# A float32 decoder trunk on one core: the down projection accumulates onto the residual held in PSUM, and one more of its weight pairs is multiplied in seven block products

## Chip, cores and metric

The kernel runs on one core of one Trainium2 chip. The metric is the device time of one execution in microseconds (us); three runs of the kernel before gave 2077.24 to 2078.20, with a median of 2077.91 us.

## What is computed

Two pre-norm residual layers over a stream `h` of 256 positions by 2048 features, all in float32. Each layer adds a mixer (sliding-window attention beside an mLSTM in the first layer, forgetting attention in the second) and then a SwiGLU feed-forward block (FFN); a last RMSNorm ends it. The change lies in the FFN:

```
def swiglu(xn, w_gate, w_up, w_down):
    return (jax.nn.silu(xn @ w_gate) * (xn @ w_up)) @ w_down
...
        h = h + swiglu(rms_norm(h, norm_ffn[layer]), w_gate[layer], w_up[layer], w_down[layer])
```

`w_gate` and `w_up` are 2048 x 5632, `w_down` is 5632 x 2048.

## The kernel before

**Numbers in two parts.** Every float32 operand is split into a part `hi`, rounded to the matrix engine's type fp32r, and the rest `lo`. A product is three matmuls into one PSUM bank, hi by hi, hi by lo and lo by hi (`three`, L508 to L511). The activations are split once and stay resident (`xh`, `xl` for the FFN's input; `mh`, `ml` for its hidden values); the weights are split as they arrive: ScalarE casts `hi` (L177, L339), VectorE subtracts `lo` (L178, L340).

**Tiles.** Weights are loaded in chunks of 256 rows by 512 columns (512 KB, `load_raw`, on SyncE's queue). The 256 positions are two halves t of 128. `pair_group` (L516) computes two column blocks of 512 at once, m = 0 and 1, for both t: four accumulators `plain[m][t]`, one PSUM bank each. It walks over pairs of k (256 rows), in an order given by a table of (kind, pair).

- A **plain pair** (kind 0) splits two chunks of 128 x 1024 and multiplies eight blocks: 24 matmuls.
- A **mixed pair** (kind 1) regards the 2 x 2 blocks of positions and the 2 x 2 blocks of weights as a block product and forms it with seven products: 21 matmuls. It needs sums of weight blocks `ta`, `tb`, `tc`, `td` (four subtractions on VectorE, L568 to L571), their split into `ht` and `lt` (two tiles each, L339 and L340), and sums of activation blocks, made once per pair and part (`sums_of`, into `sx` for the FFN's input and `sd` for its hidden values). Four of its products go into four further banks, `prods`, which all mixed pairs of a group share.

After its last mixed pair a group joins the four `prods` into the tile `c` (`combine`: one ScalarE copy L525, four VectorE additions L526 to L529).

PSUM has two pools of four banks, `pm` and `pa`. A group takes its `plain` banks from one and its `prods` from the other; the next group takes them the other way round. So a group's `plain` banks are those that the group before had as `prods`, and come free through `combine`.

**The FFN** (`ffn`, L598) runs in three parts of the hidden dimension, of 3, 4 and 4 column blocks (`PARTS`). In each part, a gate and up group per column block (eight k pairs, `ORDER`, three of them mixed) makes 512 hidden columns, which are turned, split into `mh`, `ml`, and summed for the mixed pairs of down. Then two down groups (n0 = 0 and 2) multiply the part's hidden values by `w_down`, in 6 pairs for the part of 3 blocks and 8 for the others (`DOWN`), and add into `h`. In the very last part the second down group is replaced by two plain `gemm` calls. That makes 22 gate and up groups and 11 down groups, of which 4 have six pairs and 7 have eight.

Before, a down group adds to `h` in two steps: `c` as soon as `combine` has made it (L708), then each `plain` bank when its last matmul is done (`add_out`, L353).

**Buffers.** `hi` and `lo` of whole chunks: six each (`wp`). `ht` and `lt`: two each, which is one mixed pair. Raw weights: four for plain chunks, four more for the chunks of mixed pairs. `t4`: one, for `ta` and `tb`, in the groups that pass no `halves` (the FFN's). `c`: one.

**Order.** When the kernel is built, a scheduler lays out the instructions of each engine in one sequence, and tiles carry the semaphores between the sequences. So a change in one place can move instructions in others.

Of the kernel before, what the change touches and what calls it, by code (L numbers as in the profile page):

```python
# [37 lines left out]
    6: ((0, 0), (1, 1), (0, 2), (1, 3), (0, 4), (0, 5)),  # L38
    8: ((0, 0), (1, 1), (0, 2), (1, 3), (0, 4), (1, 5), (0, 6), (0, 7)),
# [33 lines left out]
def trunk(  # L73
# [253 lines left out]
    def scrap(fp, n):  # L327
        if n % 2 == 0:
            box = fp.tile([P, 4, NB], F32, tag="c", name="box", bufs=1)
            halves = box[:, 0:2, :], box[:, 2:4, :]  # L330
        elif n == 3:
            halves = [fp.tile([P, 3, NB], F32, tag=f"sd{i}", name="box", bufs=1)[:, 0:CK, :] for i in range(2)]
# [175 lines left out]
    def three(o, ah, al, hi, lo, start, stop):  # L508
        nc.tensor.matmul(o, ah, hi, start=start, stop=False)  # L509
        nc.tensor.matmul(o, ah, lo, start=False, stop=False)  # L510
        nc.tensor.matmul(o, al, hi, start=False, stop=stop)  # L511
# [4 lines left out]
    def pair_group(fp, par, lhs, sums, mats, order, todo=(), halves=None, inner=None, raws=None):  # L516
        plain = [[bank(par, "acc") for _ in range(NT)] for _ in range(2)]
        todo = list(todo)
# [13 lines left out]
        for pos, (kind, pair) in enumerate(order):  # L532
# [4 lines left out]
            if not kind:  # L537
# [4 lines left out]
                for m, (w, c0) in enumerate(mats):  # L542
                    hi, lo = load_chunk(w, k0, c0, NB)
                    run_due(todo, pos)
                    for i, t in walk:
# [4 lines left out]
                            pos == 0 and i == 0, last and i == CK - 1,  # L550
# [3 lines left out]
            if first:  # L554
# [18 lines left out]
            for src in (ra, rb) if halves else (t4, ra):  # L573
# [8 lines left out]
            where = ((0, 0), (1, 0), (1, 1), (0, 1)) if halves else ((0, 0), (0, 1), (1, 0), (1, 1))  # L582
# [6 lines left out]
            three(plain[0][0], xb[:, t0], lb[:, t0], hg[:, 1, :], lg[:, 1, :], False, False)  # L589
            three(plain[1][0], sh[:, 3, :], sl[:, 3, :], hu[:, 1, :], lu[:, 1, :], False, False)  # L590
# [3 lines left out]
            three(plain[0][1], xb[:, t1], lb[:, t1], ht[3], lt[3], False, False)  # L594
# [4 lines left out]
    def ffn(layer, fp, sx, sd, key, todo, idx_next=None, key_next=None, finish=None):  # L599
# [6 lines left out]
        for g0, g1 in zip(PARTS, PARTS[1:]):  # L606
# [69 lines left out]
            def close(acc, n):  # L676
                if not end:
                    add_out(acc, n)
                elif idx_next is None:
                    finish(acc, n, gf)  # L680
                else:
                    add_out(acc, n)
# [8 lines left out]
            for n0 in (0, 2):  # L691
                if end and idx_next is None and n0 == 2:
                    for n in (2, 3):
                        acc = new_acc()
                        gemm(acc, m_of, wd, n * NB, NB, 0, nk, nk, skew=3 if n == 3 else 1, halved=n == 3)
                        close(acc, n)
                    continue
                plain, c = pair_group(
                    fp, 1 - n0 // 2, m_of, sums_d, [(wd, n0 * NB), (wd, (n0 + 1) * NB)], order, todo
# [5 lines left out]
                for m in range(2):  # L705
                    for t in range(NT):
                        o = h[:, t, (n0 + m) * NB : (n0 + m + 1) * NB]
                        nc.vector.tensor_tensor(out=o, in0=c[:, 2 * m + t, :], in1=o, op=ALU.add)  # L708
                for m in range(2):
                    close(plain[m], n0 + m)  # L710
# [526 lines left out]
    def finish(acc, n, gf):  # L1237
        for t in range(NT):
            half = n == 3 and t == NT - 1
            part, mean, rs = (ft[:, a, t : t + 1] for a in range(3))  # L1240
            for i in range(2 if half else 1):
                cs = slice(i * S, (i + 1) * S) if half else slice(0, NB)
                o = h[:, t, n * NB + cs.start : n * NB + cs.stop]
                nc.vector.tensor_tensor(out=o, in0=acc[t][:, cs], in1=o, op=ALU.add)
# [77 lines left out]
```

## Time and profile before

| what | value |
|---|---|
| median of 3 runs | 2077.91 us |
| span of the profiled execution | 2076.6 us |
| matrix engine (PE) busy | 2066.4 us |
| vector engine (DVE) busy | 1824.5 us |
| scalar engine (ACT) busy | 1374.7 us |
| HBM read | 408.68 MB, 198 GB/s over the span |

The span runs from the first to the last instruction of one profiled execution; the median of the runs lies 1.3 us above it. A row of the grouped view gives line, engine, operation, tile written from tiles read, shape, count, then the busy time of the group and the mean duration of one instruction. A row of the timeline gives start, duration, engine, line and operation. Two instructions that follow each other on an engine overlap at their edges, so the distance of two starts is less than the duration.

### The profile page before, as it was taken

How to read it: one execution, taken by the hardware profiler on the slowest of the kernel's cores; microseconds unless marked ns; L12 is line 12 of the kernel's file. 1: busy time of each engine (PE TensorE's matmuls, PEld its weight loads, DVE VectorE, ACT ScalarE, POOL GpSimd, SP SyncE). 2: the span in 40 equal slices, each digit the busy share in tenths (PEclk: the TensorE clock that was granted, in tenths of full speed). 3: DMA queues.
4: the chain of work that ended last, by engine and by line, in shares of the span. 5: the costliest groups of instructions: out<-in, count | busy, mean ns of one | idle time of the engine just before them, and what ended most of it. 6: DMA issues, size and time to landing. Idle time of an engine off the chain costs nothing.

```text
span 2076.6 us, 26994 instructions
## 1 busy us (share of the span) xinstructions
PE 2066.4 (100%) x9473; PEld 1715.0 (83%) x9473; DVE 1824.5 (88%) x2410; ACT 1374.7 (66%) x1736; POOL 41.7 (2%) x66
## 2 busy tenths in 40 slices
PE   9999999999999999999999999999999999999998
PEld 7878888888888888888888888888888888888887
DVE  6788769999999999999899778689999999999994
ACT  6777678765676656667676776687655667456763
POOL 1010000000000000000000001000000000000000
PEclk9999999999999999999999999999999999999999
DMA  8566577666566666666576866586665667666764
GB/s 292 172 213 188 190 247 236 203 217 206 189 230 223 205 210 205 220 212 204 185 215 204 235 193 184 156 283 220 206 205 200 213 206 234 203 202 213 220 197 138
DMA packets 309575, 434.87 MB, mean 209 GB/s; under 512 B 106412, under 2 KB 114624, under 8 KB 309312
## 3 DMA queue, kind: packets, MB, share of 16 engines
q1 hardware_dynamic: 307088, 426.27, 65.1%
q0 software_dynamic: 1632, 5.80, 0.8%
q8 instruction: 74, 1.21, 0.2%
q10 hardware_dynamic: 720, 1.09, 0.2%
q14 instruction: 61, 0.50, 0.1%
HBM read 408.68 MB, written 2.12 MB: 198 GB/s over the span
## 4 chain that ended last, share of the span: by engine, by line
PE 97%; DVE 1%; ACT 1%; DMA 1%; issue 1%; SPq 0%; POOLq 0%; POOL 0%; ACTq 0%; DVEq 0%
PE acc L510 21%; PE acc L509 21%; PE acc L511 21%; PE acc L213 5%; PE acc L212 5%; PE acc L214 5%; PE prod L509 5%; PE prod L510 5%; PE prod L511 5%; PE p L369 1%; PE po L470 1%; DMA raw<-in_w_in_odd_dram 0%; ACT s L403 0%; PE po L471 0%; DVE lo L178 0%
## 5 line engine op out<-in xcount | busy, mean ns | idle before, releaser
L177 ACT CAST hi<-raw 128x1024 fp32r<-128x1024 f32 (+3 forms) x656 | 664.8, 1028 | 440.2 <-PE acc L511 269.1
L178 DVE TENSOR_TENSOR lo<-raw,hi 128x1024 fp32r<-128x1024 f32 (+3 forms) x656 | 772.8, 1192 | 146.3 <-ACT hi L177 143.5
L510 PE MATMUL acc<-lo,xh 128*128 128x512 f32 x1254 | 488.6, 390 | 0.0
L509 PE MATMUL acc<-hi,xh 128*128 128x512 f32 x1254 | 485.9, 390 | 0.5 <-ACT hi L177 0.5
L511 PE MATMUL acc<-hi,xl 128*128 128x512 f32 x1254 | 484.8, 389 | 0.0
L510 PEld LDWEIGHTS acc<-lo,xh 128*128 128x128 f32 x1254 | 235.4, 188 | 49.4 <-DVE lo L178 0.6
L509 PEld LDWEIGHTS acc<-hi,xh 128*128 128x128 f32 x1254 | 235.2, 188 | 49.5 <-ACT hi L177 0.7
L511 PEld LDWEIGHTS acc<-hi,xl 128*128 128x128 f32 x1254 | 235.4, 188 | 48.8
L510 PE MATMUL acc<-lo,mh 128*128 128x512 f32 x437 | 169.7, 389 | 0.0
L511 PE MATMUL acc<-hi,ml 128*128 128x512 f32 x437 | 168.4, 389 | 0.0
L509 PE MATMUL acc<-hi,mh 128*128 128x512 f32 x437 | 167.9, 389 | 0.0
L339 ACT CAST hi<-raw 128x512 fp32r<-128x512 f32 x109 | 67.6, 620 | 89.4 <-PE acc L511 80.5
L213 PE MATMUL acc<-lo,mh 128*128 128x512 f32 (+1 forms) x322 | 126.3, 392 | 0.0
L212 PE MATMUL acc<-hi,mh 128*128 128x512 f32 (+1 forms) x322 | 125.8, 391 | 0.0
L214 PE MATMUL acc<-hi,ml 128*128 128x512 f32 (+1 forms) x322 | 123.7, 391 | 0.0
L340 DVE TENSOR_TENSOR lt<-t,ht 128x1024 fp32r<-128x1024 f32 x95 | 115.8, 1219 | 5.2 <-ACT ht L339 5.1
L339 ACT CAST ht<-t 128x1024 fp32r<-128x1024 f32 x95 | 99.9, 1051 | 30.7 <-PE prod L511 28.8
L339 ACT CAST ht<-raw 128x1024 fp32r<-128x1024 f32 x95 | 99.7, 1050 | 29.7 <-PE acc L511 15.0
L340 DVE TENSOR_TENSOR lt<-raw,ht 128x1024 fp32r<-128x1024 f32 x95 | 115.7, 1218 | 1.8 <-ACT ht L339 1.8
L213 PE MATMUL acc<-lo,xh 128*128 128x512 f32 (+3 forms) x288 | 99.8, 348 | 0.2 <-DVE lo L178 0.2
L214 PE MATMUL acc<-hi,xl 128*128 128x512 f32 (+3 forms) x288 | 98.1, 344 | 0.0
L212 PE MATMUL acc<-hi,xh 128*128 128x512 f32 (+3 forms) x288 | 95.9, 347 | 0.3
(363 smaller groups left out, 3448.0 us busy)
## 6 DMA issues: line engine op xcount, KB each, us to landing
raw<-in_w_gate_dram SPq DMA_DIRECT2D x176, 512.0 KB, 4.5
raw<-in_w_up_dram SPq DMA_DIRECT2D x176, 512.0 KB, 4.6
raw<-in_w_down_dram SPq DMA_DIRECT2D x176, 512.0 KB, 5.1
raw<-in_w_in_odd_dram SPq DMA_DIRECT2D x88, 512.0 KB, 4.9
raw<-in_w_in_even_dram SPq DMA_DIRECT2D x51, 512.0 KB, 5.0
raw<-in_w_out_even_dram SPq DMA_DIRECT2D x32, 512.0 KB, 5.1
raw<-in_w_out_odd_dram SPq DMA_DIRECT2D x32, 512.0 KB, 4.8
hr<-in_w_in_even_dram SPq DMA_DIRECT2D x12, 512.0 KB, 4.6
```

The lines of the kernel that those rows point to most:

```text
L177: latest[0] = nc.scalar.copy(hi[:, k, 0:n], raw[:, k, 0:n])
L178: nc.vector.tensor_tensor(out=lo[:, k, 0:n], in0=raw[:, k, 0:n], in1=hi[:, k, 0:n].bitcast(F32), op=ALU.subtract)
L212: nc.tensor.matmul(o, ah[:, ts], hi, start=(k == 0), stop=False)
L213: nc.tensor.matmul(o, ah[:, ts], lo, start=False, stop=False)
L214: nc.tensor.matmul(o, al[:, ts], hi, start=False, stop=(k == k_all - 1 and cs.stop == n))
L339: nc.scalar.copy(dst_h, src)
L340: nc.vector.tensor_tensor(out=dst_l, in0=src, in1=dst_h.bitcast(F32), op=ALU.subtract)
L369: nc.tensor.matmul(pq[j % 2][:, j // 2, :], q_of(j, b), k_of(j)[:, 0:cols], start=True, stop=True)
L470: nc.tensor.matmul(po, v_of(j, 0), tt[:, j, 0:2, :].rearrange("p c q -> p (c q)"), start=True, stop=False)
L509: nc.tensor.matmul(o, ah, hi, start=start, stop=False)
L510: nc.tensor.matmul(o, ah, lo, start=False, stop=False)
L511: nc.tensor.matmul(o, al, hi, start=False, stop=stop)
```

## The change

Six edits:

1. A down group copies its four blocks of `h` into its four `plain` banks before the first matmul (ScalarE, new L518 to L521), and the matmuls accumulate onto them; none of them starts a new sum. At the end one addition per block, `plain` + `c`, writes `h`. The addition of `c` to `h` (L708 before) and `add_out` in the down groups (L353 before) fall away.
2. In `DOWN`, a third pair of six and a fourth of eight becomes mixed, and in the group of eight the plain pair 4 moves ahead of the mixed pair 3.
3. `t4` goes. All groups now write the sums of weights in the raw tiles: `ra` holds `ta` and `td`, `rb` holds `tb` and `tc`.
4. So the split tiles hold other blocks. Before, in the FFN, the first `ht` held `ta`, `tb` and the second `tc`, `td`; now the first holds `ta`, `td` and the second `tb`, `tc`. The first is thereby used by the second and by the last of the products that take sums of weights.
5. The scrap tiles with the tags of `sd` grow to four blocks, and `sd` itself takes four pairs in place of three.
6. `finish` and `close` skip the addition where nothing is left to add.

```
 DOWN = {
-    6: ((0, 0), (1, 1), (0, 2), (1, 3), (0, 4), (0, 5)),
-    8: ((0, 0), (1, 1), (0, 2), (1, 3), (0, 4), (1, 5), (0, 6), (0, 7)),
+    6: ((0, 0), (1, 1), (1, 2), (1, 3), (0, 4), (0, 5)),
+    8: ((0, 0), (1, 1), (1, 2), (0, 4), (1, 3), (1, 5), (0, 6), (0, 7)),
 }
...
+        if base is not None:
+            for m in range(2):
+                for t in range(NT):
+                    nc.scalar.copy(plain[m][t], base(m, t))
...
-                            pos == 0 and i == 0, last and i == CK - 1,
+                            base is None and pos == 0 and i == 0, last and i == CK - 1, base is not None,
...
-            t4 = ra if halves else fp.tile([P, 2, NB], F32, tag="t4", name="t4", bufs=1)
-            ta, tb, tc_, td = (
-                (ra[:, 0, :], rb[:, 0, :], rb[:, 1, :], ra[:, 1, :])
-                if halves
-                else (t4[:, 0, :], t4[:, 1, :], ra[:, 0, :], ra[:, 1, :])
-            )
+            ta, tb, tc_, td = ra[:, 0, :], rb[:, 0, :], rb[:, 1, :], ra[:, 1, :]
...
-            for src in (ra, rb) if halves else (t4, ra):
+            for src in (ra, rb):
...
-            where = ((0, 0), (1, 0), (1, 1), (0, 1)) if halves else ((0, 0), (0, 1), (1, 0), (1, 1))
+            where = ((0, 0), (1, 0), (1, 1), (0, 1))
...
                 if not end:
-                    add_out(acc, n)
+                    return
...
-                        o = h[:, t, (n0 + m) * NB : (n0 + m + 1) * NB]
-                        nc.vector.tensor_tensor(out=o, in0=c[:, 2 * m + t, :], in1=o, op=ALU.add)
-                for m in range(2):
-                    close(plain[m], n0 + m)
+                        nc.vector.tensor_tensor(out=place(m, t), in0=plain[m][t], in1=c[:, 2 * m + t, :], op=ALU.add)
+                    close(None, n0 + m)
```

More of the change, by code (lines that the diff above doesn't have):

```diff
@@ L331, in scrap @@
         elif n == 3:
-            halves = [fp.tile([P, 3, NB], F32, tag=f"sd{i}", name="box", bufs=1)[:, 0:CK, :] for i in range(2)]
+            halves = [fp.tile([P, 4, NB], F32, tag=f"sd{i}", name="box", bufs=1)[:, 0:CK, :] for i in range(2)]
         else:
@@ L593, in pair_group @@
             three(prods[3], sh[:, 1, :], sl[:, 1, :], ht[2], lt[2], first, last)
-            three(plain[0][1], xb[:, t1], lb[:, t1], ht[3], lt[3], False, False)
+            three(plain[0][1], xb[:, t1], lb[:, t1], ht[3], lt[3], False, False, base is not None)
         if inner is None:
```

22 lines of the change are left out of this document (12 added, 10 removed).

## The prediction, made before the changed kernel ran

> **What bounds the kernel now.** I read the page first: busy time, then the chain that ended last.
>
> ```profile
> span 2076.6 us, 26994 instructions
> PE 2066.4 (100%) x9473; PEld 1715.0 (83%) x9473; DVE 1824.5 (88%) x2410; ACT 1374.7 (66%) x1736; POOL 41.7 (2%) x66
> ...
> PE 97%; DVE 1%; ACT 1%; DMA 1%; issue 1%; SPq 0%; POOLq 0%; POOL 0%; ACTq 0%; DVEq 0%
> ```
>
> The matrix engine is never idle for long: 10.2 us of the span. Matmuls overlap, so busy time hides their pace; that I take from starts in the timeline, on PE and then on VectorE, at the end of a down group:
>
> ```profile
> 1004.57 0.39 PE L511 MATMUL prod<-ht,sd 128*128 128x512 f32 x1
> ...
> 1005.03 0.39 PE L511 MATMUL acc<-ht,ml 128*128 128x512 f32 x1
> ...
> 1007.52 0.39 PE L510 MATMUL acc<-lo,mh 128*128 128x512 f32 x1
> ```
> ```profile
> 1005.00 0.69 DVE L526 TENSOR_TENSOR c<-prod,c 128x512 f32<-128x512 f32 x1 [2.26 <-PE prod L511]
> 1005.73 0.69 DVE L527 TENSOR_TENSOR c<-prod,c 128x512 f32<-128x512 f32 x1
> 1006.45 0.69 DVE L528 TENSOR_TENSOR c<-prod,c 128x512 f32<-128x512 f32 x1
> 1007.06 0.68 DVE L529 TENSOR_TENSOR c<-prod,c 128x512 f32<-128x512 f32 x1
> 1007.66 1.28 DVE L708 TENSOR_TENSOR h<-c,h 128x512 f32<-128x512 f32 x2
> ```
>
> From the start at 1004.57 to that at 1007.52 there are 13 steps in 2.95 us: one matmul is worth 0.227 us. And a reader of a bank starts 0.04 us after the last matmul's end (1004.57 + 0.39 to 1005.00). Next, the windows over the two FFN stretches (columns: PE, PE load, DVE, ACT, POOL busy, clock, DMA share, GB/s):
>
> ```profile
> 293.00:1009.00 716.00, 716.00 (x3168) 592.92 (x3167) 670.14 (x839) 469.79 (x534) 0.69 (x1) 1.00 0.66 212
> 1385.00:2025.00 640.00, 640.00 (x2829) 529.91 (x2828) 605.70 (x752) 414.41 (x457) 1.28 (x2) 1.00 0.66 211
> ```
>
> VectorE is busy for 1275.8 of 1356 us, 94.1%: the second limit is close. The waits say why it is not nearer:
>
> ```profile
> ACT hi L177 <- PE acc L511: 269.3, 187, 5.0
> ...
> DVE lo L178 <- ACT hi L177: 143.5, 166, 5.5
> ```
>
> ScalarE waits for matmuls to free `hi` tiles, and VectorE for ScalarE: both run ahead of PE until the tiles are full. PE has a lead over nothing; they have one over it.
>
> **Part 1, matmuls saved.** 29 mixed pairs of down show as 87 rows of three products each; the new tables have 4 x 3 + 7 x 4 = 40. Each of the 11 more saves three matmuls, 33 in all, and the built programs differ by just that (9301 and 9268). Gain 33 x 0.227 = **7.5 us**, on PE, which sets the end.
>
> ```profile
> L510 PE MATMUL prod<-lt,sd 128*128 128x512 f32 x87 | 33.9, 389 | 0.0
> ...
> L353 DVE TENSOR_TENSOR h<-acc,h 128x512 f32<-128x512 f32 x56 | 37.2, 683 | 4.8 <-PE acc L214 4.4 <-PE acc L511 0.4
> L708 DVE TENSOR_TENSOR h<-c,h 128x512 f32<-128x512 f32 x44 | 29.5, 684 | 0.0
> ```
>
> **Part 2, VectorE's account.** Its pace, again by starts:
>
> ```profile
> 660.83 0.68 DVE L568 TENSOR_TENSOR t<-raw 128x512 f32<-128x512 f32 x1
> 661.44 0.68 DVE L569 TENSOR_TENSOR t<-raw 128x512 f32<-128x512 f32 x1
> 662.04 1.22 DVE L340 TENSOR_TENSOR lt<-raw,ht 128x1024 fp32r<-128x1024 f32 x1
> 663.17 0.68 DVE L340 TENSOR_TENSOR sd<-s,sd 128x512 fp32r<-128x512 f32 x1
> 663.78 4.62 DVE L178 TENSOR_TENSOR lo<-raw,hi 128x1024 fp32r<-128x1024 f32 x4
> 668.32 1.22 DVE L340 TENSOR_TENSOR lt<-t,ht 128x1024 fp32r<-128x1024 f32 x1
> ```
>
> A half tile (512) takes 0.605, a whole one 1.135 us. A plain pair costs two wholes, 2.27; a mixed pair three wholes and five halves, 6.43, so one more costs 4.16, and 11 cost 45.8. The sums of activations for six more pairs (one per part) take four small additions and the `lo` of a half tile each; the small ones follow at 0.21:
>
> ```profile
> 656.11 0.29 DVE L262 TENSOR_TENSOR s<-c 128x128 f32<-128x128 f32 x1
> 656.32 0.28 DVE L264 TENSOR_TENSOR s<-c 128x128 f32<-128x128 f32 x1
> ```
>
> That is 4 x 0.2 + 0.605 = 1.4 per pair, 8.4 for six. The one addition per block in place of two saves 44 x 0.605 = 26.6. Net **+27.6 us**: the FFN then needs 1303.4 of 1348.5 us, 96.7%, if PE keeps its pace. In a six-pair down group the account is 30.95 us of VectorE (9 wholes, 15 halves in the three mixed pairs with 6 wholes more, 8 halves) against 135 x 0.227 = 30.6 of PE: there it lives on its lead.
>
> **Part 3, ScalarE.** 44 copies of `h`, and 1.6 us of casts per extra mixed pair, some 50 us in all on an engine that is two thirds busy: nothing in bulk. The write into PSUM has no row; the nearest are the copy out of it and the cast in SBUF.
>
> ```profile
> L525 ACT COPY c<-prod 128x512 f32<-128x512 f32 x40 | 23.1, 577 | 0.0
> ...
> L339 ACT CAST hi<-raw 128x512 fp32r<-128x512 f32 x109 | 67.6, 620 | 89.4 <-PE acc L511 80.5 <-ACT ht L339 4.3 <-issue 2.9
> ```
>
> I take 0.62 and keep 0.58 to 0.70 as bounds; over the five places below where it counts, that is 0.2 us down and 0.4 up. The Trainium skill ("ScalarE: Activation LUTs", section "Step-by-step: what each stage is for") holds that ScalarE reaches PSUM faster than SBUF, without a figure for this form; by it the low end would stand, 0.2 us off the sum.
>
> **Part 4, where PE will wait.** The order of the changed program differs in all FFN groups, not in down alone. Before, the last `prods` matmul of a group stands some 25 to 55 places ahead of the first `plain` matmul of the next; at the first eight-pair down group 40, or 9.07 us:
>
> ```profile
> 667.72 0.39 PE L511 MATMUL prod<-ht,sx 128*128 128x512 f32 x1
> ...
> 676.79 0.39 PE L509 MATMUL acc<-hi,mh 128*128 128x512 f32 x1
> ```
>
> After the change it is the tail of the group:
>
> ```
> 3009 L511 Matmult prod_5835<-ht_6018,sx1_2411 128x512
> 3010 L509 Matmult acc_6148<-hi_6245,mh_60 128x512
> 3011 L510 Matmult acc_6148<-lo_6246,mh_60 128x512
> 3012 L511 Matmult acc_6148<-hi_6245,ml_61 128x512
> 3013 L509 Matmult acc_6149<-hi_6158,mh_60 128x512
> ```
>
> `acc_6149` takes the bank of `prod_5835`. It needs that product's end, the first addition of `combine`, and now a copy of `h`. On ScalarE the copy stands behind the cast of an `ht` tile that the same row 3009 frees. Casts follow at 0.94:
>
> ```profile
> 656.89 1.04 ACT L339 CAST ht<-t 128x1024 fp32r<-128x1024 f32 x1
> 657.83 1.05 ACT L339 CAST mh<-c 128x1024 fp32r<-128x1024 f32 x1
> ```
>
> So: matmul 0.39, 0.04, cast 0.94, copy 0.62, 0.05, together 2.04 us; four places give 4 x 0.227 = 0.91. PE waits 1.13. Queued behind the copy is the cast of the next `hi`, and behind PE's wait everything. There are four such boundaries (the gate to down step of all eight-pair parts), 4.5 us, and one with seven places, 0.45. The rest by the same way of counting:
>
> - Turn to layer 1: the transposes of `h` that need a block with `c` stand six places (1.36 us) behind the last `prods` matmul; in between lie its end 0.43, four `combine` additions (1005.00 to 1007.66, 2.66 us) and the block's addition 0.69, 3.8 us. Wait **2.5**. Before, 48 places lay between.
> - One reuse of an `ht` tile after 3 places (0.68) where end, cast and hand-over take 1.53: 0.85. Two of an `lt` tile after 10 places (2.27) with a subtraction more (2.79): 1.0. One `hi` after 4: 0.6.
>
> These chains begin and end on PE, so no lead elsewhere shortens them: **9.9 us**. Beyond them some 40 reuses (first banks of gate groups with 7 to 9 places, `lo` and `lt` with 15 to 17, `ht` and `hi` with 9 to 11) have less than 1 us over their chain. If a quarter of them finds ScalarE or VectorE half way through an instruction of 1.05 to 1.22, that is 10 x 0.55 = **5.5 us**, an estimate from those rows.
>
> Of the rest: the raw tiles that now hold the sums are freed with the last `lt`, as `ra` was before, and SyncE loads `ra` ahead of `rb`, so the weight stream doesn't start later; no DMA is added. Without `t4` a first `ht` waits for four subtractions in place of two, 1.2 us, hidden by the lead of `lt`:
>
> ```profile
> 658.36 1.22 DVE L340 TENSOR_TENSOR lt<-t,ht 128x1024 fp32r<-128x1024 f32 x1
> ```
> ```profile
> 663.64 0.39 PE L510 MATMUL prod<-lt,sx 128*128 128x512 f32 x1
> ```
>
> Made at 659.58, read at 663.64: 4 us early. If that cover goes, 11 pairs of down lose up to 1.2 us each, 13 us; that belongs to the second rival.
>
> **Sum.** 2076.6 - 7.5 + 9.9 + 5.5 = 2084.5 us for the profiled execution's span; the median of the runs shown is 1.3 higher, and I set the forecast between, **2085**.
>
> **Rivals.**
>
> 1. *PE stays the limit (the other side).* The order is pessimistic: also in the old order matmuls with `lt` are split off and put late, and the trace shows those tiles 4 us early. If PE then arrives late at the tight places because it is itself the slow one, or the chains overlap with waits that I count twice, the 33 matmuls come out whole: 2077.9 - 7.5 = 2070.4. It decides as long as all waits stay under 7.5 us. Against it: the chains start at PE's own row.
> 2. *VectorE becomes the limit.* If it can't be pushed over today's 94.1%, the FFN takes 1303.4 / 0.941 = 1385 us in place of 1356: 2077.9 + 29 = 2107. It decides once the lead of about 4 us is used up in the down groups. For it: the six-pair groups' account; against it: the 9.9 us of waits on PE give VectorE time back.
> 3. *Gain and chains cancel*, without the queueing: 2077.9 - 7.5 + 9.9 = 2080.3, to 2077 if ScalarE's copies are early.
> 4. *The clock falls* where PE pauses. If it halved for the first pair (24 matmuls) of each down group: 11 x 24 x 0.227 = 60, 2138. The rows show a clock of 1.00 in both stretches. The Trainium skill ("TensorE: Matmul & The Clock Gate", section "HAM oscillation — how this bites in real kernels") puts the pause that does it at over some 3.4 us; the waits counted here are shorter.
>
> **Chances.** Forecast (2080.5 to 2095) 0.55; rival 1 (2070 to 2076) 0.19; rival 2 (2095 to 2110) 0.13; rival 3 (2076 to 2080.5) 0.12; rival 4 0.01. A difference of 0.2%, 4.2 us, is about what this kernel's measurement can tell: faster means under 2073.8, slower over 2082.1. Of rival 1 I count 0.15 as faster, the other 0.04, rival 3 and 0.07 of the forecast as same; slower is 0.62. The range 2072 to 2105 leaves out half of rival 1 and the end of rival 2. The part of it that is slower, 2082 to 2105, is the likeliest one's own.
>
> **What would show it.** Right: PE's idle time up by 10 to 20 us, with waits of about 1 us for `ScalarE L521` at the first down group of the eight-pair parts, one of 2 to 3 us ahead of the transposes at 1010 us, 33 fewer matmuls at an unchanged 0.227, VectorE at 95 to 96% in the FFN. Rival 1: PE idle as now, FFN stretches shorter by 7 us. Rival 2: PE waits for `lo` and `lt` all over the down groups, VectorE idle under 4%. Wrong in kind: waits on DMA, a longer matmul pace, or a change of time outside the FFN.

## The result and the profile after

The changed kernel takes **2179.51 us** (median of four runs, 2176.61 to 2184.8) against 2078.05 for the kernel before in the same job: a ratio of **1.0493, 95% interval 1.0478 to 1.0508**. The profiled execution has a span of 2177.3 us. The forecast was 2085 with a range up to 2105: the sign was right, the size was not. The page's summary of the changed kernel, then its row of cores and clock:

```profile
span 2177.3 us, 26938 instructions
PE 2102.1 (97%) x9440; PEld 1714.6 (79%) x9440; DVE 1854.0 (85%) x2462; ACT 1411.2 (65%) x1808; POOL 41.8 (2%) x66
...
PE 64%; DVE 14%; DMA 9%; ACT 6%; issue 5%; SPq 2%; ACTq 0%; POOLq 0%; POOL 0%; DVEq 0%
```
```profile
core 0: 2177.3 us, clock 0.989
```

The work came out as counted: 33 matmuls fewer (9473 to 9440), VectorE 29.5 us more (27.6 in the account). But PE idles for 75.2 us in place of 10.2, and the chain that ended last, 97% PE before, now runs through VectorE, DMA and ScalarE for 14, 9 and 6% of the span. What PE, ScalarE and SyncE's queue wait for in the changed kernel (us in total, times, longest):

```profile
PE acc L509 <- ACT acc L521: 17.9, 11, 2.6
PE prod L509 <- ACT ht L339: 8.9, 16, 2.3
PE acc L509 <- ACT mh L339: 8.9, 3, 3.3
...
PE pt L275 <- DVE h L708: 2.3, 1, 2.3
...
PE prod L510 <- DVE lt L340: 2.1, 5, 0.5
```
```profile
ACT hi L177 <- DMA raw<-in_w_down_dram: 90.9, 36, 6.2
...
ACT hi L177 <- DMA raw<-in_w_gate_dram: 57.4, 22, 8.6
```
```profile
SPq L123 <- DVE lo L178: 821.2, 383, 16.8
SPq L123 <- DVE lt L340: 420.1, 184, 15.4
SPq L647 <- ACT c L645: 81.7, 20, 5.8
```

The same rows of the kernel before, for ScalarE and for SyncE:

```profile
ACT hi L177 <- DMA raw<-in_w_down_dram: 1.2, 5, 0.3
```
```profile
SPq L123 <- DVE lt L340: 190.0, 86, 8.2
SPq L123 <- DVE raw L570: 150.8, 40, 7.6
SPq L123 <- DVE lo L340: 91.8, 30, 7.8
```

So ScalarE now waits for weights that it hardly ever waited for. SyncE's waits for `lt` subtractions have doubled, but the two other rows that freed a raw tile of a mixed pair before (L570, the subtraction `tc`, and the `lo` of L340) have fallen to 1.3 and 1.0 us: the three together were 432.6 us and are 422.4 now. The release of both tiles has moved to the last `lt`; the queue doesn't stand longer for it in total.

Outside the FFN almost nothing moved. From the first start of the matmuls of `three` (L509 to L511) in an FFN to the last lie 686.4 us before and 741.4 after in layer 0, and 644.0 before and 689.4 after in the last layer: 55.0 and 45.4 us more, 100.4 of the span's 100.7. Within the FFN, counting each matmul at 0.227 us, about a fifth of PE's lost time lies in the six-pair down groups, three fifths in the eight-pair ones, and the rest in the gate and up groups right behind a down group; the first gate and up groups of each layer (124.4 us) lose nothing. The window over the last layer's FFN after the change (columns as in the prediction):

```profile
1436.00:2125.00 689.00, 659.54 (x2830) 532.19 (x2829) 621.59 (x779) 434.59 (x495) 0.70 (x1) 0.99 0.63 196
```

VectorE is busy for 621.59 of 689, 90.2%; before it was 94.6% (605.70 of 640). That is the reading that surprised me most: VectorE has more to do, time is lost, and yet VectorE is *less* filled. In the slices about 40 us into the down groups of an eight-pair part one sees PE hold and the clock with it (windows of 2 us; the clock is the third number from the end):

```profile
1838.00:1840.00 2.00, 0.51 (x3) 0.06 (x1) 2.00 (x3) 2.00 (x3) 0.00 (x0) 1.00 0.80 252
1840.00:1842.00 2.00, 1.16 (x3) 0.98 (x4) 2.00 (x4) 0.79 (x1) 0.00 (x0) 0.72 0.78 203
1842.00:1844.00 2.00, 1.77 (x5) 0.86 (x3) 2.00 (x3) 0.00 (x0) 0.00 (x0) 0.50 0.74 216
```
```profile
1838.11 0.40 PE L511 MATMUL acc<-hi,sd 128*128 128x512 f32 x1
...
1839.75 1.04 ACT L339 CAST mh<-c 128x1024 fp32r<-128x1024 f32 x1
1840.84 0.29 PEld L509 LDWEIGHTS acc<-hi,mh 128*128 128x128 f32 x1 [2.77 <-ACT mh L339]
1840.84 0.80 PE L509 MATMUL acc<-hi,mh 128*128 128x512 f32 x1 [2.33 <-ACT mh L339]
...
1841.86 0.63 PE L509 MATMUL acc<-hi,mh 128*128 128x512 f32 x1
...
1842.29 0.63 PE L510 MATMUL acc<-lo,mh 128*128 128x512 f32 x1
...
1844.04 1.04 ACT L177 CAST hi<-raw 128x1024 fp32r<-128x1024 f32 x1 [3.25 <-DMA raw<-in_w_down_dram]
```

The hidden values come late (`mh` at 1839.75), PE pauses for 2.33 us, then starts matmuls 0.43 us apart (1841.86 to 1842.29) at a clock of 0.50, and meanwhile ScalarE waits 3.25 us for a weight tile. SyncE's timeline shows what stands in its queue upstream:

```profile
1795.12 23.11 SPq L123 DMA_DIRECT2D raw<-in_w_down_dram  x8
1821.54 5.13 SPq L647 DMA_TRANSPOSE turned<-c  x4
1826.76 23.38 SPq L123 DMA_DIRECT2D raw<-in_w_down_dram  x12
```

Four transposes wait in order for the late `c` and take 5.13 us to issue, and the next weight loads stand behind them until 1826.76. They are not what delayed the tile of 1844.04: two loads go out right behind them, and then SyncE waits 2.6 and 5.9 us for `lt` subtractions to free raw tiles, up to 1836.82. That tile's load was issued at 1838.56 and landed at 1843.94.

### The profile page after: what moved, and what is told of

It is laid out like the page before. It is cut to its first block, busy times and chain, and to the rows that moved or that the text cites. A ratio compares the mean times of both kernels' runs of the same rounds, so it can differ in the third digit from the quotient of the medians.

```text
span 2177.3 us, 26938 instructions
## 1 busy us (share of the span) xinstructions
PE 2102.1 (97%) x9440; PEld 1714.6 (79%) x9440; DVE 1854.0 (85%) x2462; ACT 1411.2 (65%) x1808; POOL 41.8 (2%) x66
## 4 chain that ended last, share of the span: by engine, by line
PE 64%; DVE 14%; DMA 9%; ACT 6%; issue 5%; SPq 2%; ACTq 0%; POOLq 0%; POOL 0%; DVEq 0%
PE acc L509 13%; PE acc L511 13%; PE acc L510 13%; DMA raw<-in_w_down_dram 6%; PE acc L213 5%; PE acc L212 5%; PE acc L214 5%; DVE lo L178 4%; PE prod L509 3%; PE prod L510 3%; PE prod L511 3%; ACT hi L177 3%; DVE lt L340 2%; DMA raw<-in_w_gate_dram 1%; DVE raw L569 1%
## 5 line engine op out<-in xcount | busy, mean ns | idle before, releaser
L177 ACT CAST hi<-raw 128x1024 fp32r<-128x1024 f32 (+2 forms) x645 | 648.5, 1026 | 421.4 <-PE acc L511 156.5
L178 DVE TENSOR_TENSOR lo<-raw,hi 128x1024 fp32r<-128x1024 f32 (+2 forms) x645 | 758.8, 1191 | 182.2 <-ACT hi L177 179.5
L511 PE MATMUL acc<-hi,xl 128*128 128x512 f32 x1254 | 486.8, 390 | 0.0
L509 PE MATMUL acc<-hi,xh 128*128 128x512 f32 x1254 | 473.8, 391 | 4.2 <-DVE c L530 2.2
L509 PEld LDWEIGHTS acc<-hi,xh 128*128 128x128 f32 x1254 | 235.4, 188 | 56.8 <-DVE c L530 3.5
L340 DVE TENSOR_TENSOR lt<-raw,ht 128x1024 fp32r<-128x1024 f32 x212 | 255.7, 1218 | 28.6 <-ACT ht L339 28.4
L511 PEld LDWEIGHTS acc<-hi,xl 128*128 128x128 f32 x1254 | 235.7, 188 | 49.3 <-issue 0.2
L339 ACT CAST ht<-raw 128x1024 fp32r<-128x1024 f32 x212 | 216.6, 1048 | 81.3 <-DVE raw L570 30.8
L509 PE MATMUL acc<-hi,mh 128*128 128x512 f32 x360 | 143.9, 409 | 29.1 <-ACT acc L521 17.9
L510 PE MATMUL acc<-lo,mh 128*128 128x512 f32 x360 | 145.1, 403 | 0.6 <-DVE lo L178 0.5
L511 PE MATMUL acc<-hi,ml 128*128 128x512 f32 x360 | 141.7, 397 | 0.0
L509 PEld LDWEIGHTS acc<-hi,mh 128*128 128x128 f32 x360 | 70.1, 195 | 52.4 <-ACT acc L521 24.7
L340 DVE TENSOR_TENSOR lo<-raw,hi 128x512 fp32r<-128x512 f32 x120 | 82.0, 683 | 6.0 <-ACT hi L339 5.9
```

Source lines behind the costliest of these rows:

```text
L177: latest[0] = nc.scalar.copy(hi[:, k, 0:n], raw[:, k, 0:n])
L178: nc.vector.tensor_tensor(out=lo[:, k, 0:n], in0=raw[:, k, 0:n], in1=hi[:, k, 0:n].bitcast(F32), op=ALU.subtract)
L339: nc.scalar.copy(dst_h, src)
L340: nc.vector.tensor_tensor(out=dst_l, in0=src, in1=dst_h.bitcast(F32), op=ALU.subtract)
L509: nc.tensor.matmul(o, ah, hi, start=start, stop=False, skip_group_check=seeded)
L510: nc.tensor.matmul(o, ah, lo, start=False, stop=False, skip_group_check=seeded)
```

## The experiments

Eighteen kernels ran. The theories named in them: **load** (VectorE has no time for more mixed pairs), **pairing** (edits 3 and 4: the sums in the raw tiles, the first split tile with the first and the last sum), **copy** (the copy of `h` into PSUM, edit 1), **lost buffer** (`t4` as a fifth tile), and later **held tile** (both raw tiles of a mixed pair are now held to the last `lt`), **queue** (loads stand behind the transposes), **neighbours** (mixed pairs next to each other) and **order** (in the built sequence the last product stands too close to the next use of its bank). The two FFN columns are the stretches explained above, each read from one profiled execution, which can lie a few us off the median; the share is VectorE's busy time in the last. `e5_seed_lo5`, `e13_load1`, `e14_load2`, `e16_seed_raw` and `e18_raw5_lo5` serve for times alone: they don't return the function's values (for `e13_load1` the reason is given below, for the others it isn't known), so what rests on one of them alone is weaker.

| run | time, us | ratio to before, 95% | FFN of layer 0, us | last FFN, us | VectorE |
|---|---|---|---|---|---|
| before | 2078 | | 686.4 | 644.0 | 94.6% |
| after | 2179.5 | 1.0478 to 1.0508 | 741.4 | 689.4 | 90.2% |
| e1_seed | 2076.8 | 0.9989 to 1.0008 | 686.4 | 644.0 | 93.3% |
| e2_raw | 2095.1 | 1.0070 to 1.0100 | 695.2 | 649.9 | 93.1% |
| e3_pair | 2119.7 | 1.0187 to 1.0218 | 706.5 | 663.9 | 91.3% |
| e4_seed_mix | 2131.8 | 1.0243 to 1.0274 | 712.7 | 659.1 | 93.5% |
| e5_seed_lo5 | 2088.0 | 1.0039 to 1.0069 | 686.4 | 644.0 | 93.3% |
| e6_split_pairs | 2155.8 | 1.0359 to 1.0390 | 725.7 | 681.6 | 92.2% |
| e7_transpose_act | 2172.6 | 1.0440 to 1.0475 | 739.0 | 686.4 | 90.6% |
| e8_no_neighbours | 2161.8 | 1.0386 to 1.0417 | 730.0 | 685.6 | 90.6% |
| e9_no_copy | 2188.5 | 1.0524 to 1.0556 | 746.7 | 691.8 | 91.6% |
| e10_raw_5 | 2098.5 | 1.0088 to 1.0116 | 699.2 | 650.5 | 93.1% |
| e11_six_only | 2078.0 | 0.9995 to 1.0012 | 687.3 | 644.7 | 94.3% |
| e12_three_mended | 2162.5 | 1.0394 to 1.0423 | 734.2 | 687.7 | 91.4% |
| e13_load1 | 2100.6 | 1.0095 to 1.0129 | 694.0 | 648.0 | 95.5% |
| e14_load2 | 2166.9 | 1.0413 to 1.0444 | 725.6 | 679.4 | 94.9% |
| e15_eight_old | 2122.5 | 1.0196 to 1.0227 | 708.5 | 665.2 | 91.3% |
| e16_seed_raw | 2086.7 | 1.0029 to 1.0059 | 690.4 | 646.3 | 92.5% |
| e17_apart_t4 | 2127.4 | 1.0221 to 1.0258 | 710.7 | 664.2 | 93.0% |
| e18_raw5_lo5 | 2164.7 | 1.0403 to 1.0439 | 726.2 | 684.2 | 91.2% |

### One part alone

`e1_seed`: the kernel before with edit 1 (and 6) alone; tables, `t4` and pairs of sums as before.

> Edit 1 alone: h copied into PSUM and accumulated onto, with the old tables, t4 and the old pairing of sums (2,6 against the changed kernel). Pairing theory (the new grouping of the sums in split tiles is what makes the groups late): 2074 to 2080 us, as before, VectorE busy some 27 us less. Load theory (the extra mixed pairs cost it): the same, 2074 to 2080. Copy theory (the copies of h stand in ScalarE's way at each seeded group): 2120 to 2170, with the matrix engine waiting for L521.

2076.8 us, the time of the kernel before within 0.2%. The copy by itself costs nothing, and the additions that it takes off VectorE (26.6 us by the account, 18.8 less busy by the page) bring nothing.

`e2_raw`: edits 3 and 4 alone. It adds and removes no instruction.

```
-            t4 = ra if halves else fp.tile([P, 2, NB], F32, tag="t4", name="t4", bufs=1)
...
+            ta, tb, tc_, td = ra[:, 0, :], rb[:, 0, :], rb[:, 1, :], ra[:, 1, :]
...
+            where = ((0, 0), (1, 0), (1, 1), (0, 1))
```

> Edits 3 and 4 alone: no t4, sums in the raw tiles, new pairing; old tables, old additions. No instruction is added. Pairing theory: most of the loss is here, 2120 to 2170 us. Lost-buffer theory (t4 was a fifth raw tile, the weights now arrive late): the same, 2120 to 2170, but with ScalarE waiting for weight loads. Load theory and copy theory: 2074 to 2082.

2095.1 us, 18 us slower, for a rearrangement of where four sums are kept.

`e3_pair`: the new pairs of sums, but `t4` kept: `t4` holds `ta` and `td`, `rb` holds `tb` and `tc`.

```
-            (t4[:, 0, :], t4[:, 1, :], ra[:, 0, :], ra[:, 1, :])
+            (t4[:, 0, :], rb[:, 0, :], rb[:, 1, :], t4[:, 1, :])
...
-            for src in (ra, rb) if halves else (t4, ra):
+            for src in (t4, rb):
```

> Edit 4 alone: t4 kept but holding ta and td, with tb and tc in rb; old tables, old additions. Pairing theory: as slow as e2_raw within 10 us. Lost-buffer theory: 2074 to 2082, as before. Load theory and copy theory: 2074 to 2082.

2119.7 us, slower than without `t4`. So the loss of a buffer alone is not it: with the buffer back and the pairs new it is worse. What fits that, though no run shows it apart: the single `t4` is now in use from the first to the last of the four subtractions and on to its `lt`, and the next pair has to wait for it.

`e9_no_copy`: the changed kernel with edit 1 taken back, so that down adds to `h` in two steps again.

```
-                    fp, 1 - n0 // 2, m_of, sums_d, [(wd, n0 * NB), (wd, (n0 + 1) * NB)], order, todo, base=place
+                    fp, 1 - n0 // 2, m_of, sums_d, [(wd, n0 * NB), (wd, (n0 + 1) * NB)], order, todo
```

> The changed kernel without its first edit: new tables, sums in the raw tiles, new pairs of sums, but down begins new sums and adds to h in two steps as before (VectorE 44 additions of 0.605 more, 26.6 us; ScalarE 44 copies of 0.59 less). Bunching theory with the copy as a link (alone the copy cost nothing, 2076.8; but where the last products stand 4 to 16 places ahead of the next group's first matmul, that matmul also waits for the copy that stands behind late casts on ScalarE; PE waits 17.9 us for L521 in the changed kernel, 11 times): time 2150 to 2168, 12 to 30 us less than 2179.5, as a down group's first matmul then waits only for combine's read. If the copies are innocent also here: 2172 to 2185. Load theory (VectorE has too much to do): 26.6 us more on VectorE make it slower, 2185 to 2210.

2188.5 us, 9 us slower than with the copy. PE's largest waits in this kernel:

```profile
PE acc L509 <- DVE c L526: 20.9, 12, 3.6
PE acc L509 <- ACT mh L339: 13.1, 4, 3.3
```

Where the changed kernel waits 17.9 us for L521, this one waits 20.9 us for `combine`'s first addition, at the same place. The copy was only the last in line; behind it stands `combine`, which waits for the last product 15.6 us in the changed kernel and 6.3 here.

### More mixed pairs

`e4_seed_mix`: the changed kernel with `t4` and the old pairs of sums (edits 3 and 4 taken back). To fit, `lo` has five tiles in place of six. `e5_seed_lo5`: `e1_seed` with five `lo` tiles, its control.

```
+        lo = wp.tile([P, CK, NB], F32R, tag="lo", name="lo", bufs=5)
```

> Edits 1 and 2 (copies of h, and the extra mixed pairs in their new order), with t4 and the old pairing; room for it from one lo tile less (5 for 6). Pairing theory: 2068 to 2085 us, most of the loss gone. Load theory: 2140 to 2180, as the changed kernel, since VectorE's account is the same. Lost-buffer theory: as the pairing theory.

> The copy of h into PSUM alone, with the old tables, t4 and the old pairs of sums, but with five lo tiles in place of six: the control for the run that had the new tables with five lo tiles (2131.8). Lost-tile theory: the missing lo tile is what cost that run its time; then this one takes 2110 to 2130, with PE waiting for lo tiles. Table theory (the extra mixed pairs cost it): the sixth lo tile is cover that is seldom used (VectorE's lo waits for ScalarE's hi, not the reverse), so 2077 to 2083, PE idle under 15 us. Between the two, what stands over 2077.4 is the tile's share and the rest of the 54 us is the tables'.

2131.8 us with the tables, 2088.0 for the control. The tile costs 10.0 us over the median of the kernel before beside it, none of it in the FFN (686.4 and 644.0). About 2122 is left for the new tables with `t4` and old pairs, 44 us over 2078; the two FFN stretches grew by 26.3 and 15.1 us. This is an upper bound: the control has the old tables, and with the new ones the fifth tile may cost in the FFN too. The six-pair down groups, which this kernel shares with the next, lose about 7 us of PE's time here and about 1.3 there.

`e11_six_only`: `e1_seed` with the new six-pair table; the eight-pair table is old.

> The copy of h into PSUM and only the six-pair table changed (a third mixed pair, three in a row), t4 and the old pairs of sums kept: 12 matmuls less, 12 x 0.227 = 2.7 us. VectorE's account in a six-pair down group is 30.95 us to 30.6 of PE, the tightest of all groups. Load theory: these groups run out of lead; 2085 to 2100, with PE idle over 15 us. Order theory (what counts is the distance between the last product and the next use of its bank, 19 to 55 places in this kernel as in the one before): the six-pair groups carry it, and 2074 to 2076 come out, under the kernel before by 2 to 3 us.

2078.0 us: the third mixed pair in six costs nothing, and the 2.7 us of its twelve matmuls don't come out either. The tightest groups by VectorE's account, 30.95 to 30.6, cost nothing as long as the sums are made as before.

`e8_no_neighbours`: the changed kernel with its mixed pairs apart, as many as before. `e17_apart_t4`: the same table in `e4_seed_mix`.

```
+    6: ((1, 0), (0, 1), (1, 2), (0, 3), (1, 4), (0, 5)),
+    8: ((1, 0), (0, 1), (1, 2), (0, 3), (1, 4), (0, 5), (1, 6), (0, 7)),
```

> The changed kernel whole, with the same number of mixed pairs in other places: in the six-pair groups mixed pairs at positions 1, 3, 5 and in the eight-pair groups at 1, 3, 5, 7, never two next to each other (the changed kernel has 2, 3, 4 and 2, 3, 5, 6). Adjacency theory (two mixed pairs in a row want four raw tiles and both ht tiles at once, and two mixed pairs cost VectorE 12.9 us where PE takes 9.5): with a plain pair between them the lead is won back, and 20 to 50 us return, to 2130 to 2160. Load theory: the sum of work counts, not its place; within 10 us of 2179.5. Pairing theory: the bunching lies inside each mixed pair, so also within 10 us.

> The kernel that had the copy, the new tables, t4, the old pairs of sums and five lo tiles (2131.8), with its mixed pairs apart: at positions 1, 3, 5 of six and 1, 3, 5, 7 of eight, as many as before. Neighbour theory (two mixed pairs in a row need both ht tiles and four raw tiles at once, and their 12.9 us on VectorE stand against 9.5 on PE): most of its 36 us in the FFN come back, 2095 to 2108. Number theory (four of eight cost what they cost, wherever they stand): 2125 to 2138. A group that begins with a mixed pair could cost something of its own at its start: then the first of each group shows it as a wait for ht or lt.

2161.8 and 2127.4 us: 18 us come back in the changed kernel, 4 where `t4` and the old pairs are kept. In the FFN stretches it is 15.2 in the changed kernel and nothing with `t4` (712.7 and 659.1 us with neighbours, 710.7 and 664.2 apart). Neighbours are not the reason for the tables' cost where the old sums are kept; as many mixed pairs placed apart cost as much.

### VectorE's load alone

`e13_load1` and `e14_load2`: `e1_seed` with one subtraction of each mixed pair done twice, or three times. In the FFN it has the same operands each time.

```
             nc.vector.tensor_tensor(out=tb, in0=rb[:, 1, :], in1=rb[:, 0, :], op=ALU.subtract)
+            nc.vector.tensor_tensor(out=tb, in0=rb[:, 1, :], in1=rb[:, 0, :], op=ALU.subtract)
```

> The kernel with the copy of h into PSUM alone (2076.8), and in each mixed pair the subtraction that makes tb is done twice with the same operands: 95 mixed pairs in the FFN, 95 x 0.605 = 57.5 us more on VectorE. With the 26.6 us that the copy saved, VectorE's account stands 30.9 over that of the kernel before, 3.3 over my 27.6 for the changed kernel (a FFN account of 96.4% at PE's pace), with no table, pair or buffer changed; the chain from raw tile to ht grows by one subtraction. Load theory (VectorE can't be pushed far over 94.1%): time 2100 to 2170, with PE waiting for lo, ht and lt all over the FFN. Structure theory (it is where the mixed pairs stand and how their sums are made, not the sum of VectorE's work): 2077 to 2088. In the built order the last product stands 15 to 48 places ahead of the next use of its bank.

> As the run before, with the subtraction of tb done three times: 115 us more on VectorE, an account 88 us over the kernel before, 100.6% of the FFN at PE's pace (1275.8 + 88.3 of 1356). VectorE is the limit by its account: at least 1364 in place of 1356, 2086; if it can't go over 94.1%, 1364 / 0.941 = 1450, 2171. Load theory: 2150 to 2200, nearly as slow as the changed kernel or slower. Structure theory: 2086 to 2110. The pair of this and the run before gives the slope of time over VectorE's account.

2100.6 and 2166.9 us. The windows over the last FFN, `e13_load1` first:

```profile
1399.00:2047.00 648.00, 645.64 (x2850) 533.88 (x2849) 619.06 (x777) 427.59 (x481) 0.70 (x1) 1.00 0.66 209
```
```profile
1436.00:2115.00 679.00, 658.09 (x2864) 539.50 (x2863) 644.44 (x822) 424.63 (x481) 0.70 (x1) 0.99 0.65 199
```

VectorE is filled to 95.5% and 94.9%. With twice the load it comes near the limit that the second rival set (94.1%; 2171 forecast for this run). The page counts 115 more VectorE instructions in `e13_load1` than in `e1_seed`, not 95: 20 mixed pairs outside the FFN have the doubled subtraction too. (There `tb` is written over one of its operands, so the second subtraction forms another sum.) Of the 22 us that it lies over `e1_seed`, 10.7 fall between the two FFN stretches. In the stretches themselves an account like the changed kernel's (1858.5 us busy against 1854.0) costs 7.6 and 4.0 us. So **load of this size, spread over all mixed pairs, is worth some 12 us to the 29 of the second rival, and it is not what costs 101**. The new tables put their load in the down groups alone; no run here does that without adding mixed pairs.

### The two together

`e16_seed_raw`: the changed kernel with both old tables. `e15_eight_old`: with the old eight-pair table alone. `e10_raw_5`: `e2_raw` with `RAWS = 5`, `t4`'s room as a fifth raw tile.

> The changed kernel with both tables as before: the copy of h into PSUM, sums in the raw tiles, new pairs of sums (2095.1 without the copy, 2076.8 with the copy alone). Adds VectorE 26.6 us less than that 2095.1 kernel. Pairing theory (first ht waits for four sums, the last products come late whatever the load): 2093 to 2100. Load theory (the late sums cost only because VectorE has no time to spare): 2077 to 2086. Sub-question: if this is near 2077 and the run before is near 2095, the six-pair table and the pairing act together as well.

> The changed kernel whole, but the eight-pair table as before (three mixed pairs of eight at 2, 4, 6); the six-pair table stays new. 21 more matmuls than the changed kernel, 4.8 us; VectorE 29.1 less (7 mixed pairs at 4.16). If the fourth mixed pair of the eight-pair groups carries the loss, alone (load) or together with the sums in the raw tiles: 2085 to 2100. If the pairs of sums and the lost t4 carry it: 2140 to 2165. From the groups of the trace (six-pair parts lost 2.3 and 0.6 us, eight-pair parts 16 to 35 each) I hold the first for likelier.

> Sums of weights in the raw tiles and the new pairs alone (it took 2095.1 with old tables and old additions), with the room of t4 given to a fifth raw tile for mixed pairs, so that the memory is that of the kernel before. Held-tile theory: before, rb was free after the four subtractions (SyncE's waits for L570, 150.8 us) and now only after the last lt, so the weight stream starts later; a fifth tile pays that back: 2077 to 2083. Pairing theory: the order of sums within the split tiles makes the cost, and a fifth tile doesn't mend it: the built order has 7 to 25 places between last product and next use of the bank in both, so 2090 to 2100.

2086.7, 2122.5 and 2098.5 us. With the copy, edits 3 and 4 cost 9 us in place of 18: VectorE's 23.9 us less of busy time fit that, as time in which late sums can be caught up. And a fifth raw tile mends nothing (2095.1 and 2098.5).

With a third mixed pair in the six-pair groups, which was free in `e11_six_only`, edits 3 and 4 cost 45. These two kernels differ in nothing else, and the pages show the same work on PE and VectorE, `e11_six_only` first:

```profile
PE 2063.7 (99%) x9461; PEld 1712.5 (82%) x9461; DVE 1819.1 (88%) x2400; ACT 1402.7 (68%) x1790; POOL 44.7 (2%) x66
```
```profile
PE 2082.3 (98%) x9461; PEld 1717.6 (81%) x9461; DVE 1819.1 (86%) x2400; ACT 1397.9 (66%) x1790; POOL 45.0 (2%) x66
```

So 44.5 us come with VectorE busy for 1819.1 us in both: more work can't be the reason. Counting each matmul at 0.227 us, the last FFN of `e15_eight_old` loses 12.4 us in the six-pair down groups and 6.0 in the gate and up groups right behind them; `e11_six_only` loses 1.2 and 0.0 there. Its window over the last FFN:

```profile
1405.00:2070.00 665.00, 652.17 (x2842) 534.41 (x2841) 607.24 (x752) 428.91 (x487) 0.71 (x1) 0.99 0.65 203
```

VectorE has no more to do than before (607.24 to 609.5 us), yet it fills 91.3% and the stretch takes 21 us longer. What acts together is the way the sums are made and the extra mixed pair.

### Mending the changed kernel

`e6_split_pairs` casts and subtracts half tile by half tile, in the old pairs; `e7_transpose_act` issues the transposes of `c` from ScalarE; `e12_three_mended` takes both and the table of `e8_no_neighbours`; `e18_raw5_lo5` has five raw tiles and five `lo` tiles.

```
+            for quad in ((ta, tb), (tc_, td)):
...
+                for b, one in enumerate(quad):
+                    split_plain(hs[:, b, :], ls[:, b, :], one)
```
```
-                        nc.sync.dma_start_transpose(turned[b][:, :, t, :], flat[:, b, t, :])
+                        nc.scalar.dma_start_transpose(turned[b][:, :, t, :], flat[:, b, t, :])
```

> The changed kernel whole, but the casts and subtractions of the sums go half tile by half tile in the old pairs (ta with tb, tc with td), though the sums still stand in the raw tiles: 4 x 128x512 in place of 2 x 128x1024 on each engine (0.605 x 2 in place of 1.135 on VectorE, 0.08 us per tile; 131 mixed pairs, some 20 us more on VectorE and as much on ScalarE in the whole kernel). In the built program the last product of a group stands 15 to 31 places ahead of the next group's first matmul into the same bank, where the changed kernel has 4 to 26 and the kernel before 24 to 55. Pairing theory (the sums that are made first and second no longer lie in one tile, so that the first product with a sum has to wait for the last sums and the products bunch at the group's end): time falls by 20 to 45 us, to 2135 to 2160, and the waits of PE for L521's copies fall under 5 us. Load theory (VectorE and ScalarE have too much to do with three and four mixed pairs): the added instructions make it slower, 2185 to 2200.

> The changed kernel whole, with one edit: the FFN's transposing DMAs of c are issued by ScalarE, not by SyncE, so that the loads of weights on SyncE no longer stand behind a transpose that waits for the late combine and silu. Queue theory (part of the loss at the gate to down step is the weight stream held up behind these transposes: ScalarE waits 91 us for tiles of w_down and 57 us for w_gate, before the change 1.2 and 6.1): these waits fall under half and the time falls by 15 to 40 us, to 2140 to 2165. Pairing and load theories: the waits for DMA follow from late raw tiles (freed by the lt subtractions), not from the transposes; the time stays within 8 us of 2179.5, or grows since ScalarE now issues the DMAs.

> The changed kernel with three edits together that each gave something back alone: half tiles in the old pairs of sums (2155.8), no two mixed pairs next to each other (2161.8), the FFN's transposes issued by ScalarE (2172.6); 23.7, 17.7 and 6.9 us less than 2179.5. In the built order the last products stand 9 to 38 places ahead of the next use of their bank, against 4 to 26. If the three mend different links of one chain, they add up or less: 2130 to 2145. If the loss lies in the waits on PE that feed one another, more than the sum comes back, 2095 to 2130. If what is left is the mixed pairs' load and the lost t4, no more than 30 us come back in all: 2148 to 2160.

> The changed kernel whole with a fifth raw tile for mixed pairs, its room taken from the sixth lo tile (which costs 10.6 us, nothing of it in the FFN of the last layer, 644.0 us with and without). Held-tile theory for the joint part (both raw tiles of a pair are held until the last lt, and with a fourth mixed pair SyncE's loads stand behind them, 420 us of its queue's waits for lt): 2130 to 2155 in spite of the lo tile, and ScalarE's waits for w_down (90.9 us) fall under 40. Order theory (the first ht waits for four sums and the last products bunch at the group's end, 4 to 27 places ahead of the next use of their bank with five tiles as with four): 2175 to 2195.

Alone they give back 23.7 us (old pairs), 6.9 (transposes) and, above, 17.7 (neighbours); the three together give 17, no more than one of them, and only 8.9 of it in the two FFN stretches; most of the rest lies behind the last FFN (45.1 us to the end for 51.9). Most of the waits only change their name. In `e12_three_mended` PE waits for

```profile
PE prod L510 <- DVE lt L340: 11.2, 11, 2.3
PE acc L509 <- ACT acc L521: 11.1, 10, 1.7
```

L521 has fallen from 17.9 to 11.1, and `lt`, 2.1 us before the mending, has taken its place. The fifth raw tile cuts ScalarE's waits for `w_down` from 90.9 us to

```profile
ACT hi L177 <- DMA raw<-in_w_down_dram: 25.2, 21, 5.0
```

and the FFN stretches go from 741.4 to 726.2 and from 689.4 to 684.2, 20.4 of the 100.4 us. So the late weight tiles, the most striking row of the profile after, are mostly a consequence: take nearly three quarters of them away, and four fifths of the time are still lost, now to other waits.

## Why the prediction was wrong

- **Matmuls saved, 7.5 us.** The count was right, and the pace outside the slow stretches too. But in `e11_six_only` 2.7 us of such a gain didn't come out, with VectorE not loaded more than before.
- **VectorE's account, +27.6.** Right in size: 29.5 by the page.
- **The copy, 0.62.** It took 25.7 us for 44:

```profile
L521 ACT COPY acc<-h 128x512 f32<-128x512 f32 x44 | 25.7, 586 | 22.6 <-DVE c L530 18.1 <-DVE c L531 4.2
```

  That is 0.586 each, near the low bound. The Trainium skill ("ScalarE: Activation LUTs", section "Step-by-step: what each stage is for"), by which ScalarE reaches PSUM faster than SBUF, is in line with that: 0.586 into PSUM against 0.620 for the cast in SBUF. The two differ in output type too, so this is weak support.
- **Chains that begin and end on PE, 9.9 us.** The places were right, the turn to layer 1 almost to the tenth (2.5 forecast, 2.4 by its own terms, 2.3 for L275), the copy's boundaries not: 4.95 forecast, 17.9 measured, 11 times. I took the products to be on time and counted places behind them; `combine` then waited 15.6 us for them, 13 times. As a mechanism it is too small by far, and the copy is no part of it (`e9_no_copy`).
- **"Without `t4` a first `ht` waits for four subtractions in place of two, 1.2 us, hidden by 4 us lead of `lt`."** This is the step that failed: the sum put edits 3 and 4 at nothing. They cost 18 us alone, 9 with the copy's relief, 44.5 with the copy and the third mixed pair of six (`e15_eight_old` against `e11_six_only`), and at least 58 with all new tables (2179.5 against the 2122 of `e4_seed_mix` less its lo tile). The price if the cover goes, 13 us, was for 11 pairs of down; but all 40 mixed pairs of down lose `t4`, and at the same 1.2 us each they would come to 48. The lead was read at one place. That VectorE at 94.6% has only 5% of its time to win a late step back fits this, but is argued.
- **The mixed pairs themselves got no term.** The sum took VectorE's 96.7% to cost no time. With `t4` and the old pairs kept, the new tables cost up to 44 us (`e4_seed_mix`), nearly all in the FFN. The third mixed pair of six alone cost nothing (`e11_six_only`).
- **"The weight stream doesn't start later."** False as a fact: before, `rb` was free after the subtractions; now both raw tiles are held to the last `lt`, and SyncE's waits for `lt` go from 190.0 to 420.1 us, in place of the waits for L570 and `lo`. By price it is the smaller part: a fifth raw tile mends nothing in `e10_raw_5` and gives back 20.4 us of the two FFN stretches in `e18_raw5_lo5`. I had listed waits on DMA as "wrong in kind"; they were there, but as an effect.
- **Rival 2, VectorE as the limit, 2107, chance 0.13.** The closest. Its cap held roughly where the sums stayed as they were: `e14_load2` 2166.9 for 2171, `e4_seed_mix` about 2122 for 2107. What it lacked is that the share itself falls: VectorE reaches 93 to 95.5% in the kernels that keep `t4` and its pairs, and 90 to 92% in those that have the third edit and the new tables. Taking the FFN's account of 1303.4 us, 94.6% gives 1378 us (22 over 1356) and 90.2% gives 1445 (89 over); the stretches grew by 100.4. That is the same loss told as a share, not its reason.
- **Rival 4, the clock, chance 0.01.** It is there in part. The mean clock fell from 0.999 to 0.989, at most 22 us of the span, after pauses of 2.3 us. The Trainium skill ("TensorE: Matmul & The Clock Gate", section "HAM oscillation — how this bites in real kernels") puts the bound at 3.4 us of idleness; here the clock showed 0.50 after a pause of 2.33 us (1840.84) that ended a stretch of smaller ones, and 1.00 after one of 2.35 us (1606.82). The measurement decides, and the length of one pause doesn't settle it. Whether these 22 us add to the loss or lie inside waits that would have come anyway, no run separates.

**What is shown and what is not.** Shown: the copy is innocent, alone and in place; the tables cost up to 44 us with the old sums; the sums in the raw tiles cost 9 to 18 alone and 58 or more on top of the tables; so they act together (9 + 44 is 53, measured 101), and in `e15_eight_old` they do so with no work added. Shown against, as the main cause: lost buffer, held raw tiles (20 of 100 us), neighbouring pairs, and the transposes. Not settled is why the sums in the raw tiles lower the share that VectorE reaches. What fits the runs is that the first `ht` of a pair can't be cast until all four sums are made, so that casts, `lt` and products of a mixed pair bunch, and each engine in turn has nothing to do and then too much. `e6_split_pairs` was to undo just that and gave 24 of the 101, with 9.4 us more on VectorE and 24.7 on ScalarE for its half tiles; that it would have given more without that work was only argued. A rival that no run tests is the built order itself: every kernel was laid out anew by the scheduler, and none keeps the order of before while it makes the sums the new way. No version beat the kernel before: `e1_seed` and `e11_six_only` equal it within 0.2%.

## What to carry to other kernels

When PE is at 100% and the next engine at 95%, don't price a longer dependency chain against the lead that one tile shows in one place, and don't put it at nothing: count every place where the chain stands, and ask how much of its time the second engine has left to catch up. Test two edits apart and together: here one cost 9 us, the other at most 44, and both 101. Where a loss has several striking waits, take them away one at a time and then together: here three edits that gave 7, 18 and 24 us gave 17 together, so none of the waits they took away was the cause by itself. And an edit that adds no instruction (where four sums are kept) can cost more than one that adds 44.

## What the runs showed of the hardware

PE's granted clock fell to 0.50 after a pause of 2.33 us that closed a stretch of smaller ones, with matmuls 0.43 us apart in place of 0.23 for some 3 us; after a pause of 2.35 us at 1606.82 it stayed at 1.00. A copy of 128x512 f32 from SBUF into PSUM on ScalarE took 0.586 us, 0.577 the other way. Four transposing DMAs on SyncE's queue took 5.13 us to issue (1821.54 to 1826.76), with the weight loads behind them; issuing them from ScalarE cut ScalarE's waits for `w_down` from 90.9 to 55.7 us and gained 6.9 us.
